# A decoder layer on one core: the last phase loads its blocks plainly and adds them on DVE, and rows of x are read first

## The chip, the cores and the metric

The kernel runs on one core of a Trainium2 chip. The metric is the device time of one execution in microseconds (us); of several executions the median is given, and less is better. The engines are named as the profile names them: PE (matrix products; PEld is its weight loads), DVE (vector), ACT (scalar), POOL, and SP, which here only issues DMAs. DMAs are issued on SP's queue or on POOL's queue.

## The reference

`x` is 2048 rows of 1024 numbers, float32. The layer is

```
h   = rms_norm(x, pre_g)                         # row by row
q, k, v, g_ret, u, g_pool = split(h @ w_in, 6)   # 1024 -> 6 * 1024
y_ret  = group_norm(retention(rope(q), rope(k), v)) * g * silu(g_ret)
y_pool = pooling(u) @ pool_w * pool_scale * silu(g_pool)
y   = concat(y_ret, y_pool) @ w_out              # 2048 -> 1024
out = x + rms_norm(y, post_g)
```

The change touches the last line, the second half of the product with `w_out`, and the first loads of the kernel.

## The kernel before, in words

**Products.** Each number of a large product is split into two parts (`hi` by an ACT cast, L144; `lo` by a DVE subtraction, L145), and each product of 128x128 by 128x512 is three matmuls (L330 to L332). On top of that, a product of two 2x2 block matrices is made with seven block products instead of eight: that is `class Unit` (L252). A unit takes four quarters of its moving operand, "11", "12", "21" and "22" (128x512 each), and forms S1 = 21+22, S2 = S1+11, S3 = 11+21 and S4 = S2+12. `load_sums` (L266) makes S1 and S3 in the DMA: SP loads one quarter into a tile (L261), and POOL then issues a second DMA that adds the other quarter to it (L263). `load_rest` loads 11, 22 and 12 plainly. `prep(i)` (L289) makes the splits, and S2 and S4 on DVE (L281).

**Order of the work.** The seven products run in the order 6, 2, 5, 7, 1 (of the next unit), 4, 3. The main loop (at the end of the kernel) writes, after each product, one step of the next unit's `prep` and, after products 1, 4 and 3, the loads of the unit after that. A helper `later(n, f)` puts work off by n such slots. A scheduler may move the instructions of an engine against each other, but keeps one program per engine and per DMA queue: each of them runs its list in order. Products 5 and 7 are accumulated in PSUM in bank "b" with product 6, and bank "b" has to be read by DVE (L348 forms quarter 22 of the result) before product 4 may write to it.

**Phases.** 1: 24 units of the mixer on half of the sequence; 2: eight `out_unit`s (L662) that write partial sums; 3: the mixer's other heads and pooling groups; 4, the last phase, eight `out_unit`s with `last=True`. The traces show the last one from about 1300 us on. There a unit fetches the partial sums (`fetch`, L684, SP), adds them (L693, DVE), lets ACT square and sum the result (L697), and two slots later `finish` (L707) makes the scale of each row (ten small DVE instructions, L134 to L139), multiplies the four quarters by it and by the gain (L723, DVE, a `scalar_tensor_tensor`), has POOL issue a DMA that adds the rows of `x` from memory (L729), and four slots after that SP stores the result (L733). The last unit (`final=True`) has no work behind it: it loads the rows of x into `xr` (L722), adds them on POOL, the last quarter on DVE (L727), and stores (L731).

**The start.** `first()` (L843) is written in a fixed order. SP loads a first block of four row tiles `xs`, a table of constants `cst`, positions `pos`, a table `col` with the gains by column, then transposed x (`b11`, `b21`) and weights `w`. ACT squares the rows (L862), DVE makes their scale and a diagonal matrix `dg` (L376), PE spreads it over the partitions (`rb`, L384), and then the loop over `made` runs: for each of eight tiles DVE scales (L932), ACT casts (L936), DVE subtracts (L940), PE multiplies (L951 to L953). Eight DVE instructions per block of positions (`angles`, all at L835) turn positions into angles, and ACT then takes sine and cosine (`trig`).

Of the kernel before, what the change touches and what calls it, by code (L numbers as in the profile page):

```python
# [9 lines left out]
F32 = mybir.dt.float32  # L10
# [5 lines left out]
P = 128  # L16
SEQ = 2048
DM = 1024
# [60 lines left out]


@with_exitstack
def layer_kernel(ctx: ExitStack, tc: tile.TileContext, x, xt, pos, wt, wut, wo, pw, cols, postg, const, out):
    nc = tc.nc

    kp = ctx.enter_context(tc.tile_pool(name="kp", bufs=1))
# [8 lines left out]
    nc.vector.memset(warm, 0.0)  # L94
    nc.scalar.activation(out=warm, in_=warm, func=AF.Silu)

    cst = kp.tile([P, C_W], F32, name="cst")
    col = kp.tile([P, 3 * KT], F32, name="col")
    ones = kp.tile([P, P], F32, name="ones")
    ident = cst[:, C_ID:C_ID + P]  # L100
    tri4 = cst[:, C_TRI:C_TRI + P].unsqueeze(1).broadcast_to([P, CPB, P])
# [17 lines left out]
    def T(name):  # L119
        return tmp.tile([P, BLK + HIST], F32, name=name, tag="t", bufs=NT)  # L120
# [34 lines left out]
    def later(i, stage):  # L155
        while len(slots) <= i:
            slots.append([])
        slots[i].append(stage)
# [93 lines left out]
    class Unit:  # L252
        def __init__(self, name, quads, uses):
            self.name, self.quads, self.uses = name, quads, uses
            self.op, self.bank = {}, {}
            self.fetch = self.part = None

        def land(self, name, q, more=None):
            t, view = X(f"{name}_{self.name}"), self.quads[q]
# [5 lines left out]

        def load_sums(self):  # L266
            self.raw = {}
            self.land("S1", "21", "22")
            self.land("S3", "11", "21")

        def load_rest(self, names):
            for q in names:
                self.land(q, q)

        def load(self):
            self.load_sums()
# [11 lines left out]

        def prep(self, i):  # L289
            raw = self.raw  # L290
            if i == 1:
                h11 = raw["11"]
                self.split(1, "11")
                self.add("S2", raw["S1"], h11, nc.vector)
            elif i == 2:
                self.add("S4", raw["S2"], raw["12"], nc.vector)
                self.split(6, "S2")
            elif i == 3:
                self.split(2, "12")
            elif i == 4:  # L300
                self.split(5, "S1")
            elif i == 5:
                self.split(7, "S3")
            elif i == 7:
                self.split(4, "22")
            elif i == 8:
                self.split(3, "S4")
# [354 lines left out]
    def out_unit(s, f0, last, final=False):  # L662
# [5 lines left out]
        def place(t, q):  # L668
            j = int(q[1]) - 1
            return t[rows[q[0]]][:, j * BLK:(j + 1) * BLK]  # L670
# [13 lines left out]
        def fetch():  # L684
            for q in ("11", "22", "21", "12"):
                parts[q] = T(f"pt{q}_{n}")[:, :BLK]
                nc.sync.dma_start(out=parts[q], in_=place(part, q))  # L687

        def total(q):
            def use(c, i):  # L690
                t = o[q] = T(f"ot{q}_{n}")[:, :BLK]
                if i:
                    nc.vector.tensor_tensor(out=t, in0=c, in1=parts[q], op=ALU.add)  # L693
                else:
                    c(t)
                k = 2 * (int(q[0]) - 1) + int(q[1]) - 1
                nc.scalar.activation(out=parts[q], in_=t, func=AF.Square, scale=1.0 / 32.0,  # L697
                                     accum_out=s2[:, k:k + 1])
                if final and q == "21":
                    finish(("22", "21"))  # L700
                elif final and q == "12":
                    finish(("11", "12"))
                elif q == "12":
                    later(2, lambda: finish(("11", "22", "21", "12")))
            return use

        def finish(quads):  # L707
            k0, nr = int(quads[0][0]) - 1, len(quads) // 2
            rows_s = slice(0, 2) if nr == 2 else slice(k0, k0 + 1)
            v = sml.tile([P, nr], F32, name=f"ov{n}{k0}", tag=f"ov{nr}")  # L710
            s3 = s2.rearrange("p (s j) -> p s j", j=2)
            nc.vector.scalar_tensor_tensor(out=v, in0=s3[:, rows_s, 0], scalar=EPS, in1=s3[:, rows_s, 1],
                                           op0=ALU.add, op1=ALU.add)
            rs = rsqrt(v, nr, f"f{n}{k0}")
            for q in quads:
                k, j = (int(q[0]) - 1 if nr == 2 else 0), int(q[1]) - 1
                t = o[q]
                row = rows[q[0]]
                spot = (slice(row * P, (row + 1) * P), slice(j * BLK, (j + 1) * BLK))
                if final:  # L720
                    xr = T(f"xr{q}_{n}")[:, :BLK]
                    nc.sync.dma_start(out=xr, in_=x[spot])  # L722
                nc.vector.scalar_tensor_tensor(out=t, in0=t, scalar=rs[:, k:k + 1], in1=pg[j],  # L723
                                               op0=ALU.mult, op1=ALU.mult)
                if final:
                    eng = nc.vector if q == "12" else nc.gpsimd
                    eng.tensor_tensor(out=t, in0=t, in1=xr, op=ALU.add)  # L727
                else:
                    nc.gpsimd.dma_start(out=t, in_=x[spot], accum_op=ALU.add)  # L729
                if final:  # L730
                    nc.sync.dma_start(out=out[spot], in_=t)  # L731
                else:
                    later(4, lambda t=t, spot=spot: nc.sync.dma_start(out=out[spot], in_=t))  # L733

        u = Unit(n, quads, {q: total(q) for q in quads})
        u.fetch, u.part = fetch, parts
        return u


# [103 lines left out]
    def first():  # L843
# [51 lines left out]
            nc.sync.dma_start(out=pi[b], in_=pos[:, b * BLK:(b + 1) * BLK])  # L895


        xs = {0: [row(0, 0)]}
        nc.sync.dma_start(out=cst, in_=const)
        load_pi(0)  # L900
        xs[0] += [row(0, st) for st in range(1, CPB)]
        nc.sync.dma_start(out=col, in_=cols)
        b11, b21, b22 = (r.pair(n) for n in ("b11", "b21", "b22"))
        b12 = [wide(f"b12{q}") for q in range(2)]
        load(b11[0], xt[0, 0])
        load_w(0, 0)
        load_w(1, 0)
        load(b11[1], xt[0, 1])
        load_w(0, 1)
        load_w(1, 1)  # L910
# [74 lines left out]
        turn = turns(0)  # L985
        for st in range(CPB):
            square(0, st, xs[0][st])
        for step in turn[:6]:
            step()
        spread(0)  # L990
        for k in (0, 1):
            split_w(k, 0)
            rest_w(k, 0)
        for step in turn[6:]:
            step()
        s11, s21 = Side("b11", b11, 0, 0, "rl"), Side("b21", b21, 0, KH, "rl")
        o = [acc(f"f{k}0") for k in (0, 1)]
        upper = {0: (0, 1), 1: (1, 1), 3: (2, 0), 4: (3, 0), 5: (2, 1), 6: (3, 1)}
        for i in made((s11, s21)):
            if i == 2:  # L1000
                rest_w(0, 1)
                rest_w(1, 1)
            elif i > 3 and i - 1 in upper:
                rest_w(*upper[i - 1])
            for k in (0, 1):
                multiply(o[k], k, i // KH, i % KH, (s11, s21)[i // KH])
            if i in upper:
                split_w(*upper[i])
            if i == 2:
                trig(0)  # L1010
        turn = turns(1)
        for step in turn[:5]:
            step()
        s12, s22 = Side("b12", b12, 1, 0, "rh"), Side("b22", b22, 1, KH, "rl")
        for st in range(CPB):
            square(1, st, xs[1][st])
        p = [acc(f"f{k}0") for k in (2, 3)]
        for i in range(KT):
            for k in (0, 1):
# [164 lines left out]
```

## Time and profile before

| what | before |
|---|---|
| median of 3 runs | 1480.18 us (1474.72, 1480.18, 1480.51) |
| the profiled execution: its time | 1476.45 us |
| its span in the trace | 1474.5 us |
| granted PE clock, mean | 0.994 of full speed |
| busy: PE, DVE, ACT, POOL | 97%, 74%, 48%, 17% of the span |
| DMA moved | 243.77 MB, 165 GB/s on the mean |

A busy PE is not PE at its peak: a matmul at the full clock follows the one before after 0.23 us, at the lower level after 0.43 us, and both count as busy. The span is divided among phases with different limits, so the shares of the whole span say little about the last phase, which is some 170 us long, or about the first 20 us.

### The profile page before, as it was taken

The page shows a single profiled execution, that of the slowest core. Times are in us where ns is not written, and L with a number is a line of the kernel's source. Part 1 is how long each engine was busy: PE and PEld are TensorE (multiplying, and loading weights), DVE is VectorE, ACT ScalarE, POOL GpSimd, SP SyncE. Part 2 cuts the span into 40 slices and gives each one's busy share as a digit, 9 for nine tenths or more (in the row PEclk, how much of TensorE's full clock was granted, in tenths as well). Part 3 has the DMA queues.
Part 4 walks back from the last instruction along what each step waited for, and adds up shares of the span by engine and source line. Part 5 has one row for each costly group of instructions (what it writes and reads, how often), then busy time and mean ns, then how long its engine had stood idle before and what let it go on. Part 6 is the DMA issues. An engine that isn't in the chain of part 4 may idle for free. (4 is left out here: it accounts for less than half of the span.)

```text
span 1474.5 us, 20756 instructions
## 1 busy us (share of the span) xinstructions
PE 1423.2 (97%) x6976; PEld 1188.4 (81%) x6976; DVE 1085.0 (74%) x2360; ACT 712.3 (48%) x1353; POOL 249.1 (17%) x335
## 2 busy tenths in 40 slices
PE   5999999999999999999999999999999999998985
PEld 3788888888888888888888888888888788877764
DVE  7997677878867788967787868687778544676665
ACT  6464565545554545745444444454446433553321
POOL 0001010211111222110111112111111222202222
PEclk9999999999999999999999999999999999999998
DMA  9135365635363768743535536444638755789976
GB/s 341 30 92 135 89 174 149 189 102 154 111 172 100 235 202 240 244 108 94 151 115 153 160 101 171 127 153 134 168 92 268 216 153 152 229 273 227 235 209 164
DMA packets 115370, 243.77 MB, mean 165 GB/s; under 512 B 14016, under 2 KB 14144, under 8 KB 115264
## 3 DMA queue, kind: packets, MB, share of 16 engines
q1 hardware_dynamic: 79296, 156.46, 32.1%
q0 software_dynamic: 35968, 86.00, 25.8%
q8 instruction: 54, 0.88, 0.3%
q14 instruction: 52, 0.43, 0.1%
HBM read 187.88 MB, written 54.53 MB: 164 GB/s over the span
## 5 line engine op out<-in xcount | busy, mean ns | idle before, releaser
L330 PE MATMUL b_o<-rh,h_o 128*128 128x512 f32 x192 | 76.3, 398 | 11.6 <-DVE ot_o L348 11.6
L331 PE MATMUL b_o<-rl,h_o 128*128 128x512 f32 x192 | 76.1, 396 | 0.7 <-DVE rl L145 0.7
L332 PE MATMUL b_o<-rh,l_o 128*128 128x512 f32 x192 | 76.0, 396 | 0.0
L330 PE MATMUL b_up<-rh,h_up 128*128 128x512 f32 x192 | 75.5, 393 | 0.0
L450 POOL DMA_DIRECT2D yd<-sg x32 | 24.1, 753 | 304.0 <-DVE sg L531 226.3
L332 PE MATMUL b_up<-rh,l_up 128*128 128x512 f32 x192 | 74.8, 390 | 0.0
L331 PE MATMUL b_up<-rl,h_up 128*128 128x512 f32 x192 | 74.8, 389 | 0.0
L330 PE MATMUL b_vg<-rh,h_vg 128*128 128x512 f32 x180 | 72.0, 400 | 0.0
L330 PE MATMUL b_qk<-rh,h_qk 128*128 128x512 f32 x180 | 71.2, 396 | 0.0
L332 PE MATMUL b_qk<-rh,l_qk 128*128 128x512 f32 x180 | 70.3, 391 | 0.1
L332 PE MATMUL b_vg<-rh,l_vg 128*128 128x512 f32 x180 | 70.4, 391 | 0.0
L331 PE MATMUL b_vg<-rl,h_vg 128*128 128x512 f32 x180 | 70.2, 390 | 0.0
L331 PE MATMUL b_qk<-rl,h_qk 128*128 128x512 f32 x180 | 70.2, 390 | 0.0
L524 ACT ACTIVATE on<-op,sh,y_o 128x128 f32<-128x128 f32 x128 | 48.2, 457 | 36.9 <-DVE sh L521 36.9
L145 DVE TENSOR_TENSOR rl<-m,rh 128x1024 fp32r<-128x1024 f32 x42 | 51.1, 1223 | 19.6 <-ACT rh L144 15.5
L263 POOL DMA_DIRECT2D S_qk<-in_wt x30 | 26.4, 907 | 170.4 <-DMA S_qk<-in_wt 119.3
L330 PEld LDWEIGHTS b_o<-rh,h_o 128*128 128x128 f32 x192 | 36.6, 191 | 21.6 <-DVE ot_o L348 13.6
L330 PE MATMUL a_o<-rh,h_o 128*128 128x512 f32 x128 | 49.9, 390 | 2.6 <-ACT x_o L338 2.6
L144 ACT CAST rh<-m 128x1024 fp32r<-128x1024 f32 x42 | 43.7, 1048 | 15.7 <-DMA m<-made 8.4
L330 PE MATMUL c_o<-rh,h_o 128*128 128x512 f32 x128 | 50.3, 393 | 0.8 <-ACT rh L144 0.8
L331 PE MATMUL c_o<-rl,h_o 128*128 128x512 f32 x128 | 50.1, 392 | 0.3 <-DVE rl L145 0.3
L332 PE MATMUL c_o<-rh,l_o 128*128 128x512 f32 x128 | 49.8, 389 | 0.0
(498 smaller groups left out, 4552.8 us busy)
## 6 DMA issues: line engine op xcount, KB each, us to landing
m<-made SPq DMA_DIRECT2D x30, 512.0 KB, 6.2
made<-c POOLq DMA_DIRECT2D x48, 256.0 KB, 3.8
yd<-sg POOLq DMA_DIRECT2D x32, 256.0 KB, 2.7
S_up<-in_wt POOLq DMA_DIRECT2D x32, 256.0 KB, 5.7
yd<-mx POOLq DMA_DIRECT2D x32, 256.0 KB, 3.1
b<-in_wo SPq DMA_DIRECT2D x32, 256.0 KB, 4.5
S_o<-yd SPq DMA_DIRECT2D x32, 256.0 KB, 3.0
S_o<-yd POOLq DMA_DIRECT2D x32, 256.0 KB, 7.5
```

The lines of the kernel that those rows point to most:

```text
L144: nc.scalar.copy(out=r32(hi), in_=val)
L145: (eng or nc.vector).tensor_tensor(out=r32(lo), in0=val, in1=hi, op=ALU.subtract)
L263: nc.gpsimd.dma_start(out=dst, in_=self.quads[more], accum_op=ALU.add)
L330: nc.tensor.matmul(o, wh, mh, start=opens and j == 0, stop=False, **more)
L331: nc.tensor.matmul(o, wh, ml, start=False, stop=False, **more)
L332: nc.tensor.matmul(o, wl, mh, start=False, stop=j == KH - 1, **more)
L450: nc.gpsimd.dma_start(out=yd[b][:, :, f, :], in_=t.rearrange("p (c t) -> p c t", c=CPB))
L524: nc.scalar.activation(out=self.on[:, c], in_=op[:, c], func=AF.Identity, scale=rs[:, i:i + 1], bias=shift[:, i:i + 1])
```

## The change

1. In the last phase a unit is `plain`: SP loads 21, 22, 11 and 12 once each; S1 and S3 are made on DVE, like S2 and S4. The two adding DMAs of POOL go, and one load of SP.
2. `finish` is divided: the scale is made one slot after the last quarter, the four products with it are spread over two slots, and the stores of the result are issued by POOL two slots later, no longer by SP four slots later.
3. In the last unit the rows of x are loaded with the partial sums; each quarter is multiplied by the gain as soon as it is there, and the scale and the rows of x come in with one DVE instruction per quarter. POOL adds nothing there.
4. At the start the four row tiles are loaded first, then one table that also holds the gains by column, and the positions come behind the first weights. Of the eight angle steps of block 0, six ran on DVE before the scale of the rows and two before the loop; now one runs before the loop, six run in it and one after it. Its sine and cosine are moved behind the squares of the second block.

```diff
@@ class Unit
+            self.plain = False
         def load_sums(self):
             self.raw = {}
+            if self.plain:
+                self.land("21", "21")
+                self.land("22", "22")
+                return
             self.land("S1", "21", "22")
             self.land("S3", "11", "21")
         def load_rest(self, names):
             for q in names:
-                self.land(q, q)
+                if q not in self.raw:
+                    self.land(q, q)
         def prep(self, i):
             raw = self.raw
-            if i == 1:
+            if i == 0 and self.plain:
+                self.add("S1", raw["21"], raw["22"], nc.vector)
+            elif i == 1:
                 h11 = raw["11"]
+                if self.plain:
+                    self.add("S3", raw.pop("21"), h11, nc.vector)
                 self.split(1, "11")
@@ out_unit
         def fetch():
...
+            if final:
+                for q in ("22", "21", "12", "11"):
+                    xr[q] = T(f"xr{q}_{n}")[:, :BLK]
+                    nc.sync.dma_start(out=xr[q], in_=x[spot(q)])
         def total(q):
...
-                if final and q == "21":
-                    finish(("22", "21"))
-                elif final and q == "12":
-                    finish(("11", "12"))
+                if final:
+                    nc.vector.tensor_tensor(out=t, in0=t, in1=pg[int(q[1]) - 1], op=ALU.mult)
+                    if q in ("21", "12"):
+                        row = q[0]
+                        rs = scales(int(row) - 1, 1)
+                        for e in (row + "2", row + "1") if row == "1" else (row + "1", row + "2"):
+                            nc.vector.scalar_tensor_tensor(out=o[e], in0=o[e], scalar=rs, in1=xr[e],
+                                                           op0=ALU.mult, op1=ALU.add)
+                            nc.sync.dma_start(out=out[spot(e)], in_=o[e])
                 elif q == "12":
-                    later(2, lambda: finish(("11", "22", "21", "12")))
+                    later(1, finish)
...
+        def finish():
+            rs = scales(0, 2)
+            def normed(q):
+                k, t = int(q[0]) - 1, o[q]
+                nc.vector.scalar_tensor_tensor(out=t, in0=t, scalar=rs[:, k:k + 1], in1=pg[int(q[1]) - 1],
                                                op0=ALU.mult, op1=ALU.mult)
-                    nc.gpsimd.dma_start(out=t, in_=x[spot], accum_op=ALU.add)
-                    later(4, lambda t=t, spot=spot: nc.sync.dma_start(out=out[spot], in_=t))
+                nc.gpsimd.dma_start(out=t, in_=x[spot(q)], accum_op=ALU.add)
+                later(2, lambda: nc.gpsimd.dma_start(out=out[spot(q)], in_=t))
+            for i, q in enumerate(("11", "22", "21", "12")):
+                later(i // 2, lambda q=q: normed(q))
@@ first
-        xs = {0: [row(0, 0)]}
+        xs = {0: [row(0, st) for st in range(CPB)]}
         nc.sync.dma_start(out=cst, in_=const)
-        load_pi(0)
-        xs[0] += [row(0, st) for st in range(1, CPB)]
-        nc.sync.dma_start(out=col, in_=cols)
...
         load_w(1, 0)
+        load_pi(0)
...
-        for step in turn[:6]:
-            step()
         spread(0)
...
-        for step in turn[6:]:
-            step()
+        turn.pop(0)()
...
-            if i == 2:
-                trig(0)
+            if i >= 2:
+                turn.pop(0)()
+        turn.pop(0)()
...
             square(1, st, xs[1][st])
+        trig(0)
```

`scales` in the new text is the first half of the old `finish`: the sum of the two squares of each row and `rsqrt`.

The order of the instructions moves in three places that matter here. The first is SP's queue in the last phase, about unit o6 (names: `21_o8` is quarter 21 of unit o8, `pt` are partial sums, `ot` the result). Before:

```order
L261 DMA S1_o6_8_13279<-yd1_90 128x512
L261 DMA S3_o6_8_13282<-yd1_90 128x512
L261 DMA 11_o6_8_13304<-yd1_90 128x512
L261 DMA 22_o6_8_13306<-yd1_90 128x512
L733 DMA out_0<-ot11_o0_8_13019 128x512
L733 DMA out_0<-ot22_o0_8_13065 128x512
L733 DMA out_0<-ot21_o0_8_13117 128x512
L733 DMA out_0<-ot12_o0_8_13140 128x512
L261 DMA 12_o6_8_13327<-yd1_90 128x512
L687 DMA pt11_o6_8_13449<-part6_99 128x512
```

The same place in the changed kernel:

```order
L262 DMA 21_o6_8_13279<-yd1_89 128x512
L262 DMA 22_o6_8_13281<-yd1_89 128x512
L262 DMA 11_o6_8_13304<-yd1_89 128x512
L262 DMA 12_o6_8_13321<-yd1_89 128x512
L697 DMA pt11_o6_8_13447<-part6_98 128x512
```

The four stores that stood between 22 and 12 are gone from SP's queue, and four loads stand where five did. The second place is POOL's queue, where the DMAs about unit o4 stood like this before:

```order
L263 DMA S1_o8_8_13463<-yd2_91 128x512
L263 DMA S3_o8_8_13466<-yd2_91 128x512
L729 DMA ot11_o4_8_13361<-in_x 128x512
L729 DMA ot22_o4_8_13429<-in_x 128x512
L729 DMA ot21_o4_8_13481<-in_x 128x512
L729 DMA ot12_o4_8_13504<-in_x 128x512
L263 DMA S1_o10_8_13647<-yd2_91 128x512
```

and stand like this now:

```order
L746 DMA ot11_o4_8_13371<-in_x 128x512
L746 DMA ot22_o4_8_13427<-in_x 128x512
L746 DMA ot21_o4_8_13479<-in_x 128x512
L746 DMA ot12_o4_8_13502<-in_x 128x512
L747 DMA out_0<-ot11_o4_8_13371 128x512
L747 DMA out_0<-ot22_o4_8_13427 128x512
L747 DMA out_0<-ot21_o4_8_13479 128x512
L747 DMA out_0<-ot12_o4_8_13502 128x512
L746 DMA ot11_o6_8_13555<-in_x 128x512
```

The stores of a unit follow its own adding DMAs, and no load of an operand is in that queue any more. The third place is DVE in the loop of the first block (`ang0` and `kk0` are the angle steps, `b11` and `b21` the tiles that are scaled and split, `wl` the low parts of weights). Before, with the first six steps far above, ahead of the scale of the rows:

```order
L878 TENSOR_TENSOR wl2_266<-w10_199,wh2_265 128x512
L835 SCALAR_TENSOR_TENSOR ang0_230<-kk0_231,ang0_230 128x512
L835 TENSOR_SCALAR ang0_230<-ang0_230 128x512
L932 SCALAR_TENSOR_TENSOR b11_0_0_188<-b11_0_0_188,col_79,rb0_259 128x512 x2
L940 TENSOR_TENSOR b11l0_273<-b11_0_0_188,b11h0_271 128x512
```

and now (a stretch inside the loop):

```order
L894 TENSOR_TENSOR wl3_296<-w11_202,wh3_295 128x512
L851 TENSOR_SCALAR kk0_229<-ang0_228 128x512
L946 SCALAR_TENSOR_TENSOR b21_0_0_186<-b21_0_0_186,cst_78,rb0_251 128x512
L954 TENSOR_TENSOR b11l1_265<-b11_1_0_185,b11h1_263 128x512
L851 TENSOR_SCALAR kk0_229<-kk0_229 128x512
L946 SCALAR_TENSOR_TENSOR b21_0_0_186<-b21_0_0_186,cst_78,rb0_251 128x512
L954 TENSOR_TENSOR b21l0_268<-b21_0_0_186,b21h0_266 128x512
L894 TENSOR_TENSOR wl4_320<-w20_206,wh4_319 128x512
L851 SCALAR_TENSOR_TENSOR ang0_228<-kk0_229,ang0_228 128x512
```

Between the tiles that PE multiplies there is now one angle step per tile.

## Rows read from the trace of the kernel before

**Rows 1.** The page's first part: busy time of each engine.
```profile
PE 1423.2 (97%) x6976; PEld 1188.4 (81%) x6976; DVE 1085.0 (74%) x2360; ACT 712.3 (48%) x1353; POOL 249.1 (17%) x335
```
**Rows 2.** Waits of PE, whole span: what waited, its releaser, total us, times, longest.
```profile
PE b_o L330 <- DVE ot_o L348: 11.6, 4, 4.5
PE a_o L330 <- ACT x_o L338: 2.6, 1, 2.6
...
PE a_qk L332 <- DVE l_qk L145: 0.6, 1, 0.6
```
**Rows 3.** Table of windows, five units: length, busy (instructions), PEclk, DMA share, GB/s.
```profile
1331.40:1356.90 25.50, 20.99 (x86) 16.88 (x85) 14.03 (x31) 7.45 (x17) 6.54 (x8) 0.93 0.93 216
1356.90:1377.20 20.30, 19.36 (x85) 15.69 (x85) 13.86 (x31) 7.53 (x17) 5.27 (x6) 1.00 0.91 234
1377.20:1396.25 19.05, 19.05 (x85) 15.77 (x85) 14.04 (x31) 7.75 (x17) 3.52 (x4) 1.00 0.92 226
1396.25:1420.70 24.45, 20.96 (x85) 16.81 (x84) 14.04 (x31) 7.37 (x17) 5.24 (x6) 0.93 0.81 208
1420.70:1442.70 22.00, 19.34 (x85) 15.69 (x85) 14.56 (x32) 7.32 (x17) 5.25 (x6) 1.00 0.87 234
```
**Rows 4.** Timeline of PE from 1344 on: start, us, instruction, idle before, releaser.
```profile
1349.52 0.50 PE L330 MATMUL b_o<-rh,h_o 128*128 128x512 f32 x1 [4.51 <-DVE ot_o L348]
...
1352.73 0.63 PE L332 MATMUL b_o<-rh,l_o 128*128 128x512 f32 x1
```
**Rows 5.** Timeline of DVE in the same unit.
```profile
1339.24 0.69 DVE L281 TENSOR_TENSOR sS_o<-S_o,11_o 128x512 f32<-128x512 f32 x1 [2.95 <-DMA S_o<-yd]
...
1343.29 0.69 DVE L281 TENSOR_TENSOR sS_o<-sS_o,12_o 128x512 f32<-128x512 f32 x1 [2.68 <-DMA 12_o<-yd]
```
**Rows 6.** Timeline of SP's queue in the same unit.
```profile
1331.95 5.67 SPq L733 DMA_DIRECT2D out<-ot_o  x4
1337.72 0.95 SPq L261 DMA_DIRECT2D 12_o<-yd  x1
```
**Rows 7.** Waits of SP's queue, 1303 to 1460: total us, times, longest.
```profile
SPq L733 <- DMA ot_o<-in_x: 70.2, 22, 13.9
```
**Rows 8.** DMA issues, 1290 to 1475: count, KB each, median us from issue to landing.
```profile
ot_o<-in_x POOLq DMA_DIRECT2D x28, 256.0 KB, 6.0
S_o<-yd POOLq DMA_DIRECT2D x13, 256.0 KB, 7.8
```
**Rows 9.** Timeline of DVE in the unit that starts at 1377.20.
```profile
1389.02 0.68 DVE L348 TENSOR_TENSOR ot_o<-b_o,x_o 128x512 f32<-128x512 f32 x1
...
1396.25 0.69 DVE L354 TENSOR_TENSOR ot_o<-c_o,u_o 128x512 f32<-128x512 f32 x1 [2.03 <-PE c_o L332]
```
**Rows 10.** Timeline of PE in the same unit: the first matmul of product 4.
```profile
1390.62 0.39 PE L330 MATMUL b_o<-rh,h_o 128*128 128x512 f32 x1
```
**Rows 11.** Timeline of DVE in the tail of the kernel.
```profile
1459.36 0.68 DVE L354 TENSOR_TENSOR ot_o<-c_o,u_o 128x512 f32<-128x512 f32 x1
...
1462.84 1.22 DVE L138 TENSOR_TENSOR t_fo<-t_fo,y_fo 128x1 f32<-128x1 f32 x1
...
1465.32 0.16 DVE L137 SCALAR_TENSOR_TENSOR t_fo<-y_fo,ovo 128x1 f32<-128x1 f32 x1
...
1467.93 1.64 DVE L727 TENSOR_TENSOR ot_o<-ot_o,xr_o 128x512 f32<-128x512 f32 x1
```
**Rows 12.** Timeline of ACT at the start: the second row tile.
```profile
9.82 1.06 ACT L862 ACTIVATE xs<-xs 128x1024 f32<-128x1024 f32 x1 [4.17 <-DMA xs<-in_x]
```
**Rows 13.** Timeline of DVE at the start.
```profile
10.07 2.14 DVE L835 SCALAR_TENSOR_TENSOR ang<-kk,ang 128x512 f32<-128x512 f32 x3
13.58 0.17 DVE L370 TENSOR_SCALAR msf<-ss 128x4 f32<-128x4 f32 x1 [1.36 <-ACT xs L862]
...
18.29 0.43 DVE L835 TENSOR_SCALAR ang<-ang 128x512 f32<-128x512 f32 x1
```
**Rows 14.** Table of windows, 40 to 50 us: busy of PE, PEld, DVE, ACT, POOL.
```profile
40.00:50.00 10.00, 10.00 (x47) 7.95 (x46) 9.90 (x17) 3.11 (x5) 0.00 (x0) 1.00 0.03 6
```

More of the change, by code (lines that the diff above doesn't have):

```diff
@@ L81, in layer_kernel @@
 @with_exitstack
-def layer_kernel(ctx: ExitStack, tc: tile.TileContext, x, xt, pos, wt, wut, wo, pw, cols, postg, const, out):
+def layer_kernel(ctx: ExitStack, tc: tile.TileContext, x, xt, pos, wt, wut, wo, pw, postg, const, out):
     nc = tc.nc
@@ L95, in layer_kernel @@
     nc.scalar.activation(out=warm, in_=warm, func=AF.Silu)
-    cst = kp.tile([P, C_W], F32, name="cst")
-    col = kp.tile([P, 3 * KT], F32, name="col")
+    cst = kp.tile([P, C_W + 3 * KT], F32, name="cst")
+    col = cst[:, C_W:]
     ones = kp.tile([P, P], F32, name="ones")
@@ L703, in use, with spot, scales @@
                 elif q == "12":
-                    later(2, lambda: finish(("11", "22", "21", "12")))
+                    later(1, finish)
             return use
-        def finish(quads):
-            k0, nr = int(quads[0][0]) - 1, len(quads) // 2
-            rows_s = slice(0, 2) if nr == 2 else slice(k0, k0 + 1)
+        xr = {}
+        def spot(q):
+            row, j = rows[q[0]], int(q[1]) - 1
+            return slice(row * P, (row + 1) * P), slice(j * BLK, (j + 1) * BLK)
+        def scales(k0, nr):
@@ L710, in finish @@
             v = sml.tile([P, nr], F32, name=f"ov{n}{k0}", tag=f"ov{nr}")
             s3 = s2.rearrange("p (s j) -> p s j", j=2)
-            nc.vector.scalar_tensor_tensor(out=v, in0=s3[:, rows_s, 0], scalar=EPS, in1=s3[:, rows_s, 1],
+            nc.vector.scalar_tensor_tensor(out=v, in0=s3[:, k0:k0 + nr, 0], scalar=EPS, in1=s3[:, k0:k0 + nr, 1],
                                            op0=ALU.add, op1=ALU.add)
[L714 to L723, printed above, removed]
-                                               op0=ALU.mult, op1=ALU.mult)
[L725 to L728, printed above, removed]
-                    nc.gpsimd.dma_start(out=t, in_=x[spot], accum_op=ALU.add)
-                if final:
-                    nc.sync.dma_start(out=out[spot], in_=t)
-                else:
-                    later(4, lambda t=t, spot=spot: nc.sync.dma_start(out=out[spot], in_=t))
@@ new lines, in scales @@
+            return rsqrt(v, nr, f"f{n}{k0}")
+        def finish():
[3 more added lines that the diff above has]
+                nc.vector.scalar_tensor_tensor(out=t, in0=t, scalar=rs[:, k:k + 1], in1=pg[int(q[1]) - 1],
+                                               op0=ALU.mult, op1=ALU.mult)
+                nc.gpsimd.dma_start(out=t, in_=x[spot(q)], accum_op=ALU.add)
+                later(2, lambda: nc.gpsimd.dma_start(out=out[spot(q)], in_=t))
+            for i, q in enumerate(("11", "22", "21", "12")):
+                later(i // 2, lambda q=q: normed(q))
@@ L735, in out_unit @@
         u = Unit(n, quads, {q: total(q) for q in quads})
-        u.fetch, u.part = fetch, parts
+        u.fetch, u.part, u.plain = fetch, parts, True
         return u
@@ L1171 @@
         "wut": c(wut),
-        "wo": c(np.asarray(w_out).reshape(FT, P, DM)), "pw": c(pw), "cols": c(cols),
-        "postg": c(np.asarray(post_norm_g).reshape(1, DM)), "const": _constants(),
+        "wo": c(np.asarray(w_out).reshape(FT, P, DM)), "pw": c(pw),
+        "postg": c(np.asarray(post_norm_g).reshape(1, DM)), "const": c(np.concatenate([_constants(), cols], axis=1)),
     }
```

## The prediction

> **What bounds the kernel now.** I read the page first: PE is busy for 97% of the span [rows 1], so only what makes PE wait, run at the lower clock, start later or leave more behind it can move the time. Next I read the waits of PE over the whole span [rows 2]. The reader is to see that they are few and that the largest of those after the start stands in the last phase: 11.6 us, in four waits, for L348, the DVE instruction that reads bank "b" before product 4 may write to it. One more, 2.6 us, stands at the border to that phase.
>
> The third view is the table of windows, cut at the ends of five units of the last phase [rows 3]. One unit takes 19.05 us without a stall and is PE busy from end to end; the others take 25.50, 20.30, 24.45 and 22.00. Against 19.05 they lose 6.45 + 1.25 + 5.40 + 2.95 = 16.05 us. That is more than the 11.6 of waits, and the PE timeline shows why [rows 4]: after the wait of 4.51 us the matmuls stand 0.43 us apart, eight or nine of them, where 0.23 is the pace elsewhere: the engine had been idle and the granted clock of that window is 0.93, so part of it ran at the lower of the two levels, 1.2 GHz. After the wait of 0.94 us in the second unit nothing of that kind shows.
>
> The fourth view is what held L348 up: the DVE timeline of that unit [rows 5]. DVE stood still for 2.95 us until the DMA of an S tile landed and for 2.68 us until quarter 12 landed. The S tile is the sum made by two DMAs, the second issued by POOL, with a median of 7.8 us from issue to landing [rows 8]. Quarter 12 was late for another reason: on SP's queue it was issued at 1337.72, right behind four stores that took from 1331.95 on [rows 6], because each store waits until the adding DMA of x has landed. Over the phase SP stood 70.2 us at those stores [rows 7].
>
> **The change, part by part.** *Loads and sums of the last phase.* Both reasons go. A unit needs four plain loads, where it had five and two adding ones, and no load stands behind a store on SP. So the 16.05 us are what can be had. In exchange DVE gets two more adds a unit, 0.69 us each [rows 5], on 14.04 busy of 19.05 [rows 3]; 15.4 still fits. What counts is whether L348 comes in time: in the unit without a stall it ended at 1389.70 and product 4 began at 1390.62 [rows 9, 10], 0.9 us later. The S1 add stands right ahead of L354, where DVE is idle for 2.03 us [rows 9], and so costs nothing if its two loads are there. The S3 add stands before the row scale, which waits for ACT's square anyway; at worst it takes all of its 0.69 from the 0.9. So no wait has to come back. Bounds: 0 (all covered) to 7 units by 0.6 = 4 us, if about that much is missing in each. I take 1.0, nearer to the lower end because the one clean unit [rows 9] has room, and because its loads were the ones of the other units too.
>
> *Stores by POOL.* They wait for the adding DMAs of their own unit and nothing stands behind them in POOL's queue but the same work of the next unit. No operand hangs on that queue now. What hangs on them is the reuse of result tiles: a tile of two units on can be written when the store has read it. Two landings of about 6.0 us [rows 8] and the issues come to some 15 to 17 us from L723 on; a unit takes 19.05. I put it at 0 and keep the other end as a rival. The Trainium skill has two rules here, which speak against each other: "DMA: Bandwidth & Descriptors", section "Issuing engine by pattern", gives simple stores to Sync and calls that path generally faster; section "Issuing engines are not separate DMA queues" says that issuing from several engines saves only sequencer time, usually small. By the first rule alone these 28 stores would get dearer, and by the second moving them would win next to nothing; but the row of 70.2 us [rows 7] is time in which SP's queue stood with loads behind it, so by the trace the place in the queue is what a store costs here.
>
> *The tail.* After L354 (1459.36) the old tail ran until 1467.93 + 1.64 = 1469.57 [rows 11]. Within it two tiny instructions took 1.2 us each while POOL was adding (one is shown, 1.22), others of that kind 0.16, the last add took 1.64, where DVE's adds elsewhere take 0.69 [rows 5, 11]. The new tail has no POOL work. Stepping through it: the last square is done by about 1461.0; ten tiny instructions at 0.2 apart, two chains woven together, and four instructions of 0.7 end at 1466.5 to 1467.2. So the last stores leave 2.4 to 3.1 us earlier; what follows them, 4.9 us to the span's end, stays. I take -2.8.
>
> *The start.* Two effects with opposite signs. The row tiles come first, so the squares end earlier: ACT waited 4.17 us for the second row tile [rows 12], which had the constants and positions ahead of it, and the scale of the rows began at 13.58 [rows 13]. What can be saved is bounded by 0 (the queue is slow in its first microseconds, whatever is asked for) and by the 4.17; from the bytes that are no longer ahead of the rows (0.4 MB) I get 1.1 to 2.7 and take 1.7. Against that stand the angle steps. Six ran while DVE waited for the rows, and two more while PE spread the scale; they cost nothing. Now seven are inside or behind the loop. Three `scalar_tensor_tensor` took 2.14 us one behind another [rows 13], and a `tensor_scalar` takes 0.43: woven between other instructions 4 by 0.62 and 3 by 0.38, 3.6 us (3.5 to 4.2 by how much overlaps). Is DVE on the path there? The table of windows shows it busy for 9.90 of 10 us from 40 to 50 [rows 14], as it is nearly all the way from 20 to 70, and the first wait of PE behind that is for DVE's `l_qk`, 0.6 us [rows 2]. So what is added to DVE reaches PE. Net: 3.6 - 1.7 = +1.9 us, slower. Between its ends, 4.2 - 1.1 and 3.5 - 2.7: +3.1 and +0.8.
>
> *The border to the last phase.* The 2.6 us wait for L338 [rows 2] follows ACT casts that wait for data of another kind (`made`); fewer DMAs there may help a little. Bounds 0 and -2.6, or +2 if the new S3 add delays a split; taken: -0.3. The middle phases keep their order: 0.
>
> The sum, against the profiled execution's 1476.45: -16.05 + 1.0 - 2.8 + 1.9 - 0.3 = -16.25, thus **1460.2 us**, 1.3% below the median of 1480.18. That execution was 3.7 us under the median; the spread of the three runs, 5.8 us, is what stalls by late DMAs would give, and without them the runs should sit near the profiled one. I say 1460.
>
> **The rivals.** *A, half of the stalls stay.* L348 then waits for DVE itself: the adds take the 0.9 us of room and a load or a partial sum lands late as before. For it: DMA share over 0.8 in all five windows [rows 3], and POOL's stores are added to the queue with the longer landing. Against it: three of seven loads fewer. Half of 16.05 back: 1460 + 8 = 1468. *B, the start does not lose,* because the rows come 2.7 us earlier and ACT or PE covers the steps: 1457 or a little less. *C, slower than before: the stores on POOL close a loop.* L723, adding DMA, store, free tile, and the subtractions and sums that write such tiles (u, x, ot) are in one ring. If the two landings take over 19.05 us a unit instead of 15 to 17, the ring sets the pace: from a store landing of some 9 us on, every unit stalls. A long stall costs as at 1349, 6.45 us with the slow matmuls [rows 3, 4]; in all seven units 45, and the sum is 1460 + 45 = 1505; in five of them 1492. For it: a row of DMAs issued by POOL has a median of 7.8 us already [rows 8]. Against: that one is the second half of a pair in the fullest stretches, and the traffic falls. *D, it doesn't do what it says:* DMAs take as long because the 16 engines are full, not because of the queue, and the waits for the S tile turn into waits for 21 and 22: about 1476.
>
> **How the numbers follow.** Forecast 0.64, A 0.14, B 0.08, C 0.06, D 0.08. A measurement of this kernel tells about 0.5% (7.4 us) from no change, so faster means under 1472.8 and slower over 1487.6. Faster: the forecast, B and nearly all of A, 0.84. Same: D and a little of A and C, 0.10. Slower: the rest of C, 0.06. The range from 1453 (B, with all of the wait at the border gone) to 1472 (A with its stalls above half) leaves out C, D and a little at the ends.
>
> **What would show it.** Right: no PE wait for L348 above 1 us in the last phase, units of 19.1 us, granted clock 1.00 in all of them; no SP wait at stores; in the tail no DVE instruction of one column above 0.2 us; DVE's row scale before 12.5 us, but PE's `a_qk` wait at about 72.5 us. Wrong: DVE waits for `21_o` or `22_o` (D), PE waits behind tiles that a POOL store holds (C), or PE reaching `a_qk` before 70.5 us (B).

## The result, and the profile after

The changed kernel takes 1458.8 us (median of 4 runs, 1455.96 to 1461.06), the kernel before 1479.55 in the same runs (1474.72 to 1480.51): a ratio of 0.9864, with an interval of 0.984 to 0.9887. The forecast was 1460.0 and faster. The span of the profiled execution went from 1474.5 to 1457.6 us, by 16.9; the sum in the prediction was 16.25. How far the terms of that sum agree one by one is the subject of the rest.

The waits of PE over the whole span of the changed kernel, the answer to [rows 2]:

```profile
PE rb L394 <- DVE dg L386: 12.5, 1, 12.5
PE c_o L340 <- DVE x_o L323: 1.9, 1, 1.9
PE a_qk L342 <- DVE l_qk L145: 1.8, 1, 1.8
PE f L967 <- DVE b21l L954: 1.7, 3, 0.8
...
PE a_o L340 <- ACT x_o L348: 1.1, 2, 0.7
```

The row that led [rows 2], 11.6 us for the DVE instruction in front of product 4 (L348 there, L358 now), is gone altogether. The 2.6 us at the border fell to 0.4; the other wait of that row, 0.7, stands near the end, at 1428.99. New is a wait of 1.9 us for `x_o`; it stands at 1439.80, in the last unit.

The table of windows, cut at the end of each unit of the last phase (the instruction that was L354 and is L364), the answer to [rows 3]:

```profile
1330.45:1349.49 19.04, 19.04 (x85) 15.77 (x84) 14.97 (x33) 7.72 (x17) 6.94 (x10) 1.00 0.96 241
1349.49:1368.53 19.04, 19.04 (x85) 15.77 (x84) 15.06 (x33) 7.72 (x17) 5.73 (x8) 1.00 0.83 229
...
1387.57:1406.61 19.04, 19.04 (x85) 15.77 (x84) 15.06 (x33) 7.72 (x17) 5.75 (x8) 1.00 0.80 224
1406.61:1430.46 23.85, 23.19 (x102) 18.88 (x101) 14.46 (x32) 7.57 (x17) 6.29 (x9) 1.00 0.78 224
1430.46:1447.48 17.02, 14.57 (x55) 10.93 (x53) 11.44 (x28) 3.43 (x10) 5.76 (x8) 0.90 0.53 123
1447.48:1457.60 10.12, 0.00 (x0) 0.00 (x0) 6.68 (x29) 0.72 (x2) 0.00 (x0) 0.63 0.28 104
```

Four units in a row (the one left out is the same) take 19.04 us each, at clock 1.00, though the DMA engines are as full as before in the first of them (0.96). DVE is busy for 15.0 us of a unit, 1 more than in [rows 3]: the two adds. Then one unit takes 23.85. The reader should ask what is different about the second unit from the end; the DVE timeline and SP's queue at that place say it:

```profile
1429.03 0.69 DVE L707 TENSOR_TENSOR ot_o<-b_o,pt_o 128x512 f32<-128x512 f32 x1 [4.98 <-DMA out<-ot_o]
1430.46 0.69 DVE L364 TENSOR_TENSOR ot_o<-c_o,u_o 128x512 f32<-128x512 f32 x1 [0.74 <-DMA out<-ot_o]
...
1438.97 0.68 DVE L323 TENSOR_TENSOR x_o<-c_o,pt_o 128x512 f32<-128x512 f32 x1
```
```profile
1413.56 14.49 SPq L701 DMA_DIRECT2D xr_o<-in_x  x4
```

A sum of DVE that needs nothing but PE's result and a partial sum stands 4.98 us and is released by the landing of a *store*: it had no tile to write to. At 1413.56 SP begins to issue the four loads of x for the last unit, and needs 14.49 us for it, because they too must wait for tiles. They take four of the 16 result tiles, right when the last two units need them. PE then waits for `x_o`, and runs the matmuls behind it 0.43 us apart:

```profile
1439.80 0.70 PE L340 MATMUL c_o<-rh,h_o 128*128 128x512 f32 x1 [1.92 <-DVE x_o L323]
1440.30 0.63 PE L341 MATMUL c_o<-rl,h_o 128*128 128x512 f32 x1
1440.72 0.63 PE L342 MATMUL c_o<-rh,l_o 128*128 128x512 f32 x1
```

The tail on DVE, the answer to [rows 11], and the start on ACT, DVE and PE, the answer to [rows 12, 13]:

```profile
1447.48 0.68 DVE L364 TENSOR_TENSOR ot_o<-c_o,u_o 128x512 f32<-128x512 f32 x1
...
1450.48 1.42 DVE L719 SCALAR_TENSOR_TENSOR ot_o<-ot_o,y_fo,xr_o 128x512 f32<-128x512 f32 x2
...
1453.16 1.42 DVE L719 SCALAR_TENSOR_TENSOR ot_o<-ot_o,y_fo,xr_o 128x512 f32<-128x512 f32 x2
```
```profile
5.71 1.06 ACT L878 ACTIVATE xs<-xs 128x1024 f32<-128x1024 f32 x1 [0.19 <-DMA xs<-in_x]
```
```profile
9.53 0.17 DVE L380 TENSOR_SCALAR msf<-ss 128x4 f32<-128x4 f32 x1 [8.31 <-ACT xs L878]
```
```profile
69.74 0.50 PE L342 MATMUL a_qk<-b11h,l_qk 128*128 128x512 f32 x1 [1.76 <-DVE l_qk L145]
```

The scale of the rows begins at 9.53 and not at 13.58, 4.05 us earlier. At the first unit's low part PE stands at 69.74; in the kernel before the same matmul started at 70.51. So of the 4.05 only 0.77 are left by then. (The other executions with the same start, e1, e3 to e6, e11 and e13 below, have this matmul at 69.81 to 70.66.)

With the positions of the same instruction in both traces the 16.9 us can be laid out along the span. Each number is by how much the changed kernel gained (-) or lost (+) since the line above.

| up to | before, at | after, at | change in this stretch | forecast |
|---|---|---|---|---|
| first low part (L332 / L342) | 70.51 | 69.74 | -0.8 | +1.9 |
| x_o of the last unit that only writes partial sums (L338 / L348) | 1266.06 | 1267.21 | +1.9 | 0 |
| the next x_o, behind the border | 1299.83 | 1298.82 | -2.2 | -0.3 |
| end of the second unit (L354 / L364) | 1331.44 | 1330.45 | 0.0 | 0 |
| end of the unit second from the end | 1442.72 | 1430.46 | -11.3 | -15.05 |
| end of the last unit | 1459.36 | 1447.48 | +0.4 | 0 |
| end of the span | 1474.5 | 1457.6 | -5.0 | -2.8 |

The -11.3 are -16.1 from the stalls and +4.8 in the one unit of 23.85. (The partial sums, from some 1136 us on, stand right ahead of the last phase, behind both halves of the mixer; the list of phases ahead of the prediction has the second and the third the wrong way round. No term rests on it.)

### The profile page after: what moved, and what is told of

Same layout as the page of the kernel before. It is cut to its first block, busy times and chain, and to the rows that moved or that the text cites. A ratio compares the mean times of both kernels' runs of the same rounds, so it can differ in the third digit from the quotient of the medians.

```text
span 1457.6 us, 20725 instructions
## 1 busy us (share of the span) xinstructions
PE 1422.4 (98%) x6976; PEld 1186.4 (81%) x6976; DVE 1091.5 (75%) x2379; ACT 714.3 (49%) x1353; POOL 245.6 (17%) x344
## 5 line engine op out<-in xcount | busy, mean ns | idle before, releaser
L342 PE MATMUL b_o<-rh,l_o 128*128 128x512 f32 x192 | 75.0, 391 | 0.0
L342 PE MATMUL b_up<-rh,l_up 128*128 128x512 f32 x192 | 74.8, 390 | 0.0
L342 PE MATMUL b_qk<-rh,l_qk 128*128 128x512 f32 x180 | 70.3, 391 | 0.0
L342 PE MATMUL b_vg<-rh,l_vg 128*128 128x512 f32 x180 | 70.3, 391 | 0.0
L144 ACT CAST h_o<-sS_o 128x512 fp32r<-128x512 f32 x48 | 29.7, 621 | 53.5 <-PE c_o L341 14.8
L342 PE MATMUL c_o<-rh,l_o 128*128 128x512 f32 x128 | 50.0, 391 | 0.0
```

What stands on the lines that cost most here:

```text
L144: nc.scalar.copy(out=r32(hi), in_=val)
L342: nc.tensor.matmul(o, wl, mh, start=False, stop=j == KH - 1, **more)
```

## The experiments

The theory after reading this: the plain loads ended the stalls, the stores on POOL little of it; the early loads of x gave back 5 us; the tail's own gain is 3 us of DVE work; the start is worth about nothing, because the angle steps sit on DVE's way to 70 us. Each kernel below was timed beside the kernel before on the same chip, but not all on one chip; so kernels are best compared by their ratios.

**e1: the rows of x of the last unit go to operand tiles.** From the changed kernel:

```diff
-                    xr[q] = T(f"xr{q}_{n}")[:, :BLK]
+                    xr[q] = X(f"xr{q}_{n}")
```

> The changed kernel, but the rows of x of the last unit are loaded into operand tiles, which nobody needs by then, and not into result tiles. Theory: in the changed kernel four early loads of x hold result tiles, so the sum of quarter 21 of the unit before waits 5.0 us for a store and the last two units take 40.9 us where 36.2 would do; that wait goes, and the time falls by 4 to 5 us, to about 1454. Rival: the stores on POOL are themselves too slow for the ring of result tiles; the wait for a store stays and the time is 1459 within 1.5.

Measured: 1453.66 us (1451.49 to 1453.77), ratio 0.9836 (0.9821 to 0.9851). The ends of the last two units:

```profile
1405.67 0.69 DVE L364 TENSOR_TENSOR ot_o<-c_o,u_o 128x512 f32<-128x512 f32 x1 [0.83 <-PE c_o L342]
1424.71 0.69 DVE L364 TENSOR_TENSOR ot_o<-c_o,u_o 128x512 f32<-128x512 f32 x1 [0.82 <-PE c_o L342]
...
1441.59 0.68 DVE L364 TENSOR_TENSOR ot_o<-c_o,u_o 128x512 f32<-128x512 f32 x1
```

19.04 and 16.88 us where the changed kernel had 23.85 and 17.02: 5.0 us by the traces, as expected (by the ratios, 0.0028, some 4), and no wait for a store is left. This is the best version of the study, together with e6, e10 and e12, which can't be told from it by time: from 1300 us on PE waits for nothing.

**e2: the old start.** The order of the first loads, the places of the angle steps and of sine and cosine as in the kernel before. One thing stays as changed: the gains by column are part of the table of constants.

> The changed kernel with the old start (order of the first loads and places of the angle steps as before). Theory: the earlier rows give 4.1 us and the angle steps take back 3.3 of them by 70 us, so undoing both costs 0.8: the first product starts at about 20.1 us, the first product of a unit gets its low part at 70.5, and the time is 1459 to 1460. Rival: the 1.9 us that the changed kernel loses between 75 and 1290 us belongs to the new start; then the time falls to about 1457.7.

Measured: 1459.06 us (1457.25 to 1461.16), ratio 0.9872 (0.9856 to 0.9889); the changed kernel had 0.9864. At the start the waits of PE are those of the kernel before, with the first product late and the wait for the low part short (near the end they are like those of the changed kernel):

```profile
PE rb L394 <- DVE dg L386: 16.2, 1, 16.2
...
PE a_qk L342 <- DVE l_qk L145: 0.6, 1, 0.6
```

So the start, as a whole, is worth less than these runs can tell. The 1.9 us that the changed kernel lost between 70 and 1266 us do not belong to it either: at the x_o row of 1266 us this kernel stands at 1267.03, e1 at 1266.61, e3 at 1264.72 and e4 at 1267.87. Counted from the first low part, the kernel before needs 1195.55 us to that row, the changed one 1197.47, e2 1196.85, and all executions of this study lie between 1194.9 and 1197.6: the middle of the kernel differs by 2.7 us from execution to execution, with the same code.

**e3: the old tail.** The last unit as in the kernel before: late loads of x, a product by gain and scale, adds on POOL and DVE.

> The changed kernel with the last unit ended as before (late loads of x, adds on POOL). Theory: the end after the last sum of a quarter gets 4.6 us longer (15 us where it is 10), and the 4.7 us that the early loads cost in the last two units are saved, so the time stays at 1459 within 1.5, with no wait of a sum for a store. Rival: the early loads cost nothing and the tail alone counts: 1463.4.

Measured: 1455.39 us (1454.74 to 1456.55), ratio 0.9852 (0.9837 to 0.9867). Neither number was met in us. By the ratios it is some 2 us faster than the changed kernel (0.9864), but the intervals overlap, so that it takes as long as the changed kernel, as expected, is not ruled out. The trace gives the reason in two places.

```profile
1439.46 0.68 DVE L364 TENSOR_TENSOR ot_o<-c_o,u_o 128x512 f32<-128x512 f32 x1
...
1442.94 1.22 DVE L138 TENSOR_TENSOR t_fo<-t_fo,y_fo 128x1 f32<-128x1 f32 x1
...
1448.03 1.63 DVE L739 TENSOR_TENSOR ot_o<-ot_o,xr_o 128x512 f32<-128x512 f32 x1
```

The old tail takes 10.2 us on DVE from the last sum, as it did before, against 7.1 in the changed kernel: 3.1 us are the value of the new one, with the slow tiny instructions and all. But from the last DVE instruction to the end of the span it is 3.1 us here, where the kernel before had 4.9. That 1.9 us was not the tail's way of computing, for it is gone with either tail. Most of it is POOL's last DRAIN, an instruction at the end of the program: in the kernel before it is 6.42 us long and ends 4.2 us after DVE, 1.6 us after SP's last; in e3 it is 3.17 us long and ends 0.9 us after DVE, before SP. Why it is shorter there, the runs don't show. And the 5.2 us of the early loads are saved. So the new tail as it was written cost more (5.2) than it gave (3.1).

**e4 and e13: the stores on SP.** The loads stay plain. e4 is from the changed kernel, e13 from e1:

```diff
-                later(2, lambda: nc.gpsimd.dma_start(out=out[spot(q)], in_=t))
+                later(4, lambda: nc.sync.dma_start(out=out[spot(q)], in_=t))
```

> The changed kernel, but the stores of the last phase are issued by SP, four slots later, as before; the loads stay plain. Theory: quarter 12 is again issued behind stores that wait for the adding DMAs; SP stands over 40 us at stores, DVE waits for 12 and PE for L358 in two to four units, about 8 us in all: 1465 to 1469. Rival: the S tiles made by two DMAs were the whole cause; 1457 to 1461 and no wait of PE for L358 above 1 us.

> The kernel of e1_xr_in_x with the stores on SP, four slots later. Theory: the plain loads alone take away all but one or two of the stalls, the stores on POOL take those; in the trace the last phase is 3 to 4 us longer than e1's, with a wait of DVE for a landing behind stores, and the time is 1456 to 1458 (ratio 0.985 to 0.987). Rival: without the early loads of x in result tiles the stores on SP cost nothing: the ratio of e1, 0.9836.

Measured: e4 1462.21 us, ratio 0.9895 (0.988 to 0.991), between the two numbers; e13 1458.67 us (1456.77 to 1460.17), ratio 0.9877 (0.986 to 0.9895), against 0.9836 for e1, a little more than expected. e4 still has the early loads of x; e13 against e1 is the clean pair. In e13 SP's queue and DVE show

```profile
SPq L747 <- DMA ot_o<-in_x: 47.1, 23, 7.7
```
```profile
DVE sS_o L287 <- DMA 22_o<-yd: 6.4, 1, 6.4
```

and five units lie between these two sums (L364 of the second unit and of the last but one):

```profile
1329.37 0.69 DVE L364 TENSOR_TENSOR ot_o<-c_o,u_o 128x512 f32<-128x512 f32 x1 [0.83 <-PE c_o L342]
...
1428.43 0.69 DVE L364 TENSOR_TENSOR ot_o<-c_o,u_o 128x512 f32<-128x512 f32 x1 [0.23 <-PE c_o L342]
```

SP still stands 47 us at the stores, but only one load, a quarter 22, came too late by it, and one unit took 24.6 us (the next only 17.3). The five units take 99.06 us, 3.9 more than five of 19.04; by the ratios the loss is 6 us. So the order on SP's queue is worth 4 to 6 us and not the half of the stalls that [rows 6, 7] suggested. The landing of a store is the same from either queue, a median of 4.6 us on POOL in e1 and 4.7 for the same 28 stores on SP in e13; an issue takes POOL 0.56 us and SP 0.33.

**e5: S tiles by two DMAs again.** From e1, `u.plain` stays false; the stores stay on POOL.

> The kernel of e1_xr_in_x (the changed one with the rows of x in operand tiles), but S1 and S3 are made by two DMAs again, the second issued by POOL; the stores stay on POOL. Theory: with the stores on SP the stalls were only a fourth of the old ones, so most of the old loss is the S tiles and the traffic of seven loads; DVE waits for them in at least three units, PE for L358, and the time is 8 to 14 us over e1's, 1461 to 1468 (ratio to before 0.989 to 0.994). Rival: it was the order on SP's queue, and half of the gain comes with the stores alone: 1453 to 1457.

Measured: 1470.43 us (1467.65 to 1471.55), ratio 0.9941 (0.9925 to 0.9957): 15 us (by the ratios) to 17 (by the medians) over e1, somewhat more than expected. PE and DVE wait as in the kernel before:

```profile
PE b_o L340 <- DVE ot_o L358: 10.4, 3, 5.8
PE a_o L340 <- ACT x_o L348: 1.8, 1, 1.8
```
```profile
DVE sS_o L287 <- DMA S_o<-yd: 15.8, 6, 5.0
```
```profile
1332.20 0.69 DVE L364 TENSOR_TENSOR ot_o<-c_o,u_o 128x512 f32<-128x512 f32 x1 [0.53 <-PE c_o L342]
...
1440.66 0.69 DVE L364 TENSOR_TENSOR ot_o<-c_o,u_o 128x512 f32<-128x512 f32 x1 [0.83 <-PE c_o L342]
```

With the stores out of the way the S tiles alone bring back most of the loss: 10.4 us of waits against 11.6, and 13.3 us in the five units (108.46 us) where the kernel before lost 16.1. The wait at the border comes back too (1.8 us; in the changed kernel 0.4), and with it the stretch between the two rows of x_o at the border takes 33.0 us, 33.8 in the kernel before and 31.1 to 31.9 in all executions with plain loads: it hung on the same traffic. Whether it is the pair of DMAs behind one tile or the seven transfers in place of four, e5 doesn't part. The load on the DMA engines alone is not it: the stalled units here have shares of 0.80 to 0.93 at 223 to 230 GB/s, the changed kernel's first full unit 0.96 at 241 GB/s without a stall. In the units the two parts, 13.3 here and 3.9 in e13, come near the 16.1 of both together. The trace of the kernel before had said as much, in the waits of DVE from 1300 to 1460, about two to one:

```profile
DVE sS_o L281 <- DMA S_o<-yd: 9.0, 4, 3.0
...
DVE sS_o L281 <- DMA 12_o<-yd: 4.3, 2, 2.7
```

**e6: the stores five slots late,** `later(2` to `later(5` for POOL's stores, from e1.

> The kernel of e1_xr_in_x, but POOL issues the stores five slots after the adding DMAs and not two, some 8 us later. Theory: result tiles are written again two units on, and there 4 to 5 us are left after the store has landed; so the ring closes, x or u waits 3 to 4 us for a store in four or five units, the matmuls behind it run slow for a while, and the time is 1466 to 1479. Rival: other tiles come free first and the ring has more room than 8 us: under 1456.

Measured: 1454.6 us, ratio 0.9837. That says nothing on the ring: the stores were not later. POOL's queue holds only the adds and the stores of each unit in turn, so a slot more or less moves nothing; a store that was to be 8 us later was issued at 1362.82, and the one of the changed kernel at 1363.08.

**e11: the ring made short in all units.** The rows of x of the last unit are loaded into four result tiles during the second unit and held to the end (from e1).

> The kernel of e1_xr_in_x, but the rows of x of the last unit are loaded into four result tiles early in the last phase and held there to the end, so that nearly all units have 12 result tiles where they had 16. Theory: four tiles fewer cost in each unit what they cost in the last two units of the changed kernel, 4 to 5 us with the slow matmuls, in five or six units: 20 to 30 us over e1, 1474 to 1484, about the time of the kernel before. Rival: the ring settles after the first unit and the stores keep up: under 1462.

Measured: 1497.56 us (1495.03 to 1499.32), ratio 1.0122 (1.0088 to 1.0157), 42 (by the ratios) to 44 us over e1 and slower than the kernel before: much more than the 20 to 30 expected.

```profile
PE a_o L340 <- ACT x_o L348: 21.7, 6, 5.6
```
```profile
DVE ot_o L712 <- DMA out<-ot_o: 47.5, 6, 8.9
```
```profile
1314.86 0.69 DVE L364 TENSOR_TENSOR ot_o<-c_o,u_o 128x512 f32<-128x512 f32 x1
...
1468.46 0.69 DVE L364 TENSOR_TENSOR ot_o<-c_o,u_o 128x512 f32<-128x512 f32 x1
```

Each of six units waits for a store, 7.9 us on DVE, and takes 24 to 27 us. The six take 153.6 us, in e1 110.6 (1314.10 to 1424.71): 7.2 us a unit. That is rival C of the prediction, near its price (6.45 a unit), brought about by four tiles. With 16 tiles the ring has room; with 12 it sets the pace.

**e7: the table second.** From the changed kernel, the table of constants (182 KB) is loaded behind the first row tile.

> The changed kernel with the table of constants loaded second, ahead of row tiles 2 to 4; the positions stay behind the weights. Theory by bytes: the table is 182 KB against 512 KB of a row tile, so the rows come under 0.7 us later and the scale of the rows begins at 9.5 to 10.2 us. Rival: the table itself holds the rows up, whatever its size, since in the kernel before the second row tile came 4 us late with 0.4 MB ahead of it: 11.5 us or later.

Measured in one run, 1462.82 us: the second row tile is squared at 8.02 us (5.71 in the changed kernel), and the scale of the rows begins at 11.78; in all kernels with the rows first it was 9.5 to 10.5.

```profile
8.02 1.06 ACT L878 ACTIVATE xs<-xs 128x1024 f32<-128x1024 f32 x1 [2.62 <-DMA xs<-in_x]
```

The rival's number. A table of a third of a row tile's size holds the next tile up by 2.3 us. Why, these runs don't show.

**e8: six angle steps left out** (from e1).

> The kernel of e1_xr_in_x without six of the eight angle steps of block 0 (the sine and cosine of its angles are left uncomputed, their tables hold something else). Theory: DVE is what PE waits for until 70 us, so 3.3 us less on DVE end the 1.8 us wait for the low part of the first unit and most of the 1.7 us inside the loop: PE starts that unit 3 us earlier, at about 66.7 us, and the time is about 1451. Rival: PE waits there for something else too (weights, casts), and less than 1.5 us come of it.

Measured: 1451.04 us (1450.97 to 1453.02), ratio 0.9817. From the first product to the first low part PE needs 50.7 us (16.81 to 67.53) and 53.7 in e1 (16.95 to 70.66), 3.0 less, and its wait there is 0.9 us, not 1.8. So the steps cost 3 us on the way to 70 us.

**e10 and e12: steps on ACT.** From e1, the first three angle steps are ACT instructions; in e10 in both blocks, in e12 only in block 0.

```diff
-        return [op(ts, out=ang, in0=pi, scalar1=cst[:, C_INVF:C_INVF + 1], scalar2=None, op0=ALU.mult),
+        return [op(act, out=ang, in_=pi, func=AF.Copy, scale=cst[:, C_INVF:C_INVF + 1]),
...
```

> The kernel of e1_xr_in_x, and the first three of the eight angle steps of each of the first two blocks are done by ACT, not DVE (those of block 0 right ahead of the loop, where ACT waits 2.8 us for DVE). Theory: DVE is what PE waits for until 70 us; of block 0 two steps leave the path (0.8 us), of block 1 three (1.3 us), so PE's wait for the low part at 70 us falls from 1.8 to under 0.8 and the time by 1 to 2 us against e1, to a ratio of 0.9825 or a little under. Rival: ACT's casts in the loop come later by as much, and nothing is won: ratio 0.9836.

> As e10_act_steps, but only block 0's first three angle steps are on ACT; block 1 stays on DVE. Theory: in e10 the three steps of block 1 stood on ACT ahead of the squares of block 1, DVE waited 2.7 us for those and so lost what it had won; with block 0 alone DVE reaches the scale of block 1 without a wait, 0.8 us earlier than in e1 against the first matmul, PE's wait at 70 us falls to about 1.0, and the ratio is 0.983 or a little under. Rival: DVE is not what holds PE there, and the wait stays 1.8.

Measured: e10 1454.84 us, ratio 0.9836 (0.981 to 0.9863); e12 1452.74 us, ratio 0.9837 (0.9822 to 0.9851). Nothing was won in e10, because DVE met ACT in the second block:

```profile
35.66 0.17 DVE L380 TENSOR_SCALAR msf<-ss 128x4 f32<-128x4 f32 x1 [2.66 <-ACT xs L879]
```

In e1 the same instruction starts at 35.64 without a wait; counted from the first product, PE in e10 even reaches the first low part 0.8 us later than in e1. In e12 it starts at 34.56, and PE's wait at 70 us falls to

```profile
PE a_qk L342 <- DVE l_qk L145: 1.3, 1, 1.3
```

From the first product on, PE stands 0.8 us earlier there than in e1, as expected (the wait itself was put at 1.0). It can't be told from e1 by time.

## Why the prediction was right, and where it was not

*Loads and sums: right.* The 16.05 us of [rows 3] came back whole: the units from 1330 on take 19.04 us, up to the one that the early loads hit, and e5 shows that it is the loads and sums that do it. The residual of 1.0 for missing room in front of L348 was not needed: the S1 add hides where DVE waited for PE, as the prediction said (2.03 us in front of L354 [rows 9], 0.83 or less in front of L364 now).

*Stores on POOL: the price of 0 was right, the reading of their worth too high.* The prediction took quarter 12's place behind four stores [rows 6, 7] for the second reason of the stalls. With plain loads 47 us of waiting on SP cost 4 to 6 us (e13), and without them the moved stores win little (13.3 us of stalls in e5, 16.1 before). A wait of a DMA queue counts by who needs the load behind it, not by its length. Of the two rules of the Trainium skill, "DMA: Bandwidth & Descriptors", section "Issuing engine by pattern", that simple stores are faster from Sync is seen here in the issue (0.33 us on SP, 0.56 on POOL) and not in the landing (4.7 us on SP, 4.6 on POOL). The same page of the Trainium skill, in section "Issuing engines are not separate DMA queues", calls the sequencer time that starting a DMA takes usually small. The 4 to 6 us here are not such time: they come from SP's queue, which stood in order at stores while loads waited behind them.

*The tail: right in its work, wrong in its bounds.* Forecast -2.8 by DVE's steps; the traces show -3.1 on DVE (10.2 to 7.1 us) and 1.9 more between DVE's last instruction and the end of the span. The sentence that failed is "4.9 us to the span's end, stays"; the prediction had not asked what those 4.9 us were (e3).

*The early loads of x: not priced.* The prediction costed the steps of the last unit and left out that its four loads, now issued with the partial sums, take result tiles. It had named the ring of tiles (rival C), and put it down to slow stores alone; C's sign, a wait of PE behind a tile that a POOL store holds, is there in the last two units. The price was 5.2 us against e3 and 5.0 against e1 (in e2 and e7, which keep the early loads, the last two units take 43.0 and 42.6 us where e1 takes 35.9, so 7 us); e1 takes it away and e11 shows the whole ring closed. This is the term that was missing.

*The start: one term right, the other at less than half its size.* The angle steps were put at 3.6 us; the traces have 3.3 (4.05 less 0.77), and leaving six out gives 3.0 (e8). But the gain of the rows was put at 1.7, worked out from bytes; it was 4.05 in the profiled execution and 3.1 to 4.05 in all kernels with the new order, near the upper bound that the row itself had given [rows 12]. So at the 70th microsecond the start is worth -0.8 in the profiled execution and -0.7 to +0.2 in the others with the same start (69.81 to 70.66 against 70.51), near nothing where +1.9 was forecast. The prediction's sign for rival B, PE at `a_qk` before 70.5 us, was there in the profiled execution (69.74); over whole runs neither can be told from nothing (e2).

*The border: -2.2 for -0.3.* The bound of -2.6 was there; e5 ties it to the traffic of the S tiles. The prediction had named this ("fewer DMAs there may help a little") and sized it too small.

So the main term was right by its mechanism, but that the sum came within 1 us was luck, because its errors cancel: +5.2 for the early loads and +1.9 of scatter in the middle stand against 2.7 at the start, 2.2 in the tail, 1.9 at the border and 1.0 of residue.

## What to carry to other kernels

A load that is issued earlier takes its tile earlier: before moving it, count whose tiles it takes and who writes to that ring next, and give it tiles that nobody needs any more. When a change removes several causes of one stall, undo each alone before crediting it: here the queue with 70 us of waiting was worth 4 to 6, and the sums made by pairs of DMAs most of the 16. At the start of a kernel, price the order of the first loads from the wait in the row, not from their bytes.

## What the runs showed of the hardware that was not expected

A 182 KB table in front of three row tiles delayed the next of them by 2.3 us, where the core was moving 0.3 to 0.4 MB per microsecond (e7, one run; in the kernel before, with the positions behind the table, that tile came 4 us later). A store from a result tile lands as fast from POOL's queue as from SP's (4.6 us in e1, 4.7 in e13). And with unchanged code the middle 1200 us vary by 2.7 us between executions, more than the whole start is worth.
